# The low parts of the feed-forward down weights: a VectorE subtraction against a negated ScalarE copy and an adding DMA

## The chip, the cores and the metric

The kernel runs on one core of a Trainium2 chip. The metric is the device time of one execution in microseconds (us). In the names of the engines PE is TensorE (matmul), DVE is VectorE, ACT is ScalarE, POOL is GpSimd and SP is SyncE; "PEld" is the weight load of PE. DMAs are issued by SP, ACT or POOL, each with a queue of its own.

## What is computed

One inference step of a two-layer decoder trunk, for a prompt of 512 tokens and 8 sequences of 4 new tokens each, so 544 token columns in all. Layer 0 mixes tokens with a convolution module, layer 1 with stick-breaking attention. Each mixer is followed by the same gated feed-forward block, and that block is what the change touches:

```
def conv_ffn(h, past, w_gate, w_up, w_dw, b_dw, w_down):
    g = h @ w_gate
    ext = jnp.concatenate([past, g], axis=1)
    g_conv = causal_dwconv(ext, w_dw, b_dw)
    out = (jax.nn.silu(g_conv) * (h @ w_up)) @ w_down
    return out, ext[:, -(FFN_CONV_WIDTH - 1):]
```

The model width is 1024 (8 chunks of 128), the inner width D_FF is 2816 (22 chunks of 128). All data are float32.

## The kernel before

**Split products.** Each matrix product is made of two rounded parts per operand: `whi` is the weight rounded to the matmul format (a copy on ACT, line 369), `wlo` is the rest, weight minus `whi` (a subtraction on DVE, line 372). The activations have the same two parts (`XH`/`XL`, `TH`/`TL`, `HH`/`HL`). A product of one 128x128 block is then three matmuls: whi by high, whi by low, wlo by high. They stand on lines 459 to 461, 700 to 702, 1343 to 1345, 1543 to 1545 and 1970 to 1972.

**Weights.** A ring of two buffers `raw` holds 256 columns of a weight, loaded by a DMA from DRAM (line 332). From it `W.prep` makes one "slot" after another, a pair `whi`, `wlo` in a ring of five buffers. When a slot has been used, `W.free` drops it and prepares the slot five places on. When the last slot of a raw buffer has its `wlo`, the load of a new raw buffer is issued. In the program's listing below, slots carry their number: `whi74` and `wlo74` are slot 74.

**The feed-forward block.** `ffn(l, ...)` runs the 22 inner chunks in passes of 4, 6, 6 and 6 (`PASSES`). Within a pass the gates and ups of the next chunks alternate with the down products of the pass before. The gates and ups of the last three passes use four slots for two chunks ("a quad", kinds 0, 2, 3, 4 of the specs): a scheme with seven instead of eight block products, written in `products` (from line 1535 on):

```
mm(a, s1, 4, lambda: Tn(3), False, [("T", 1, 0), ("T", 1, 1)])
used(s1)
put("keep 22", a)
put("22", y)
mm(a, s2, 4, lambda: B(1, 1), False, bk(1, 1))
```

Each `mm` is 12 matmuls into one PSUM bank. The bank `a` goes on being added to, and its value is copied out in between: `put("keep 22", a)` is, for a gate, a copy of 240 columns and one of 32 columns (8x4) on ACT (lines 1579 and 1581), for an up one copy of 272 columns (line 1611). The next `mm` into `a` has to wait until that has been read. The down products use slots of kind 0 and 1 with 4 or 6 chunks (`nk`), and add to the residual on DVE (line 1634). Behind the block follows the last pass's down product: in layer 0 as `Wide.stream`, in layer 1 as `add_group`, both through `gemm` (lines 459 to 461).

**What sets the order.** Within the block the order is not the order of the code: each step is handed to `Plan.op` with an engine, a cost, and the names that it reads and writes. `Plan.run` then plays these costs through and emits the instructions in the order of that play, engine by engine. Each engine runs its own list strictly in that order. A matmul depends on `("slot", n)`, so the cost and place of the steps that write this name decide where the planner puts the matmuls. Waits for a DMA are told to the planner as steps on an engine of their own name, such as `raw{r}` with 5.0.

Of the kernel before, what the change touches and what calls it, by code (L numbers as in the profile page):

```python
# [13 lines left out]
AF = mybir.ActivationFunctionType  # L14
ALU = mybir.AluOpType
PSUM = bass.MemoryType.PSUM

P = 128
D = 1024
NC = D // P  # L20
# [18 lines left out]
SPLIT_BUFS = 5  # L39
# [185 lines left out]
def tile_trunk(  # L225
# [9 lines left out]
    dve, act, pool, pe = nc.vector, nc.scalar, nc.gpsimd, nc.tensor  # L235
# [20 lines left out]
    raws = []  # L256
# [59 lines left out]
    class Ring:  # L316
# [26 lines left out]
                nc.sync.dma_start(out=self.raw[self.nraw][:, k, cols], in_=src[:, k, cols])  # L343
            self.nraw += i

        def prep(self, later=None, halves=False):


            if self.nprep >= len(specs):
                return  # L350
            r, kind, last, nk = specs[self.nprep]
            more = self.more is not None
            home, bufs = (self.more, 1) if more else (ring, SPLIT_BUFS)
            i = self.nprep if more else ""
            hi = home.tile([P, NC, P], F32R, tag=f"whi{i}", name=f"whi{self.nprep}", bufs=bufs)
            lo = home.tile([P, NC, P], F32R, tag=f"wlo{i}", name=f"wlo{self.nprep}", bufs=bufs)
            self.w[self.nprep] = (hi, lo, nk)
            self.nprep += 1
            n = nk
            if kind < 2:  # L360
                src = self.raw[r][:, :nk, kind * P:(kind + 1) * P]
            elif kind == 4:
                n = nk // 2
                src = self.raw[r][:, n:, P:]
            else:
                src = self.sums[r].rearrange("p a k c -> p (a k) c") if kind == 2 else self.raw[r][:, :, 0:P]

            def high(k):
                act.copy(hi[:, k, :], src[:, k])  # L369

            def low(k=slice(0, n)):
                dve.tensor_tensor(lo[:, k, :], src[:, k], hi[:, k, :], op=ALU.subtract)  # L372
                if last:
                    del self.raw[r]
                    self.load()

            if halves:
                return [lambda f=f, k=k: f(k) for k in (slice(0, n // 2), slice(n // 2, n)) for f in (high, low)]
            high(slice(0, n))
            if later is None:  # L380
                low()
            else:
                later.insert(min(LATER, len(later)), low)
# [2 lines left out]
            del self.w[self.nfree]  # L386
            self.nfree += 1

        def free(self, later=None):
            self.drop()  # L390
            self.prep(later)

    W = Ring()

# [18 lines left out]
    def pcol(row, c):  # L413
        return prm[:, c, row:row + 1]
# [242 lines left out]
    for i in range(2):  # L657
        ch0 = (PE_CHUNKS[0] + i * len(PE_CHUNKS) // 2) * P
        for m in range(8):
            nj = min(4, CW - 4 * m)  # L660
            pool.dma_start(out=trow[i][m * n_g:(m + 1) * n_g, :nj * 32].rearrange("g (j h) -> g j h", j=nj),
                          in_=conv_w_dw[0, 4 * m:4 * m + nj, ch0:ch0 + n_g * 32].rearrange("j (g h) -> g j h", h=32))


    plan = Plan(E_CONV, 0.12)
# [382 lines left out]
    for c in range(0, NC, 2):  # L1048
# [9 lines left out]
        for cc in range(2):  # L1058
            plan.op("act", 0.33, lambda c=c, cc=cc, pt=pt: act.copy(
                ext_s[:, c + cc, :, 0:PAST], pt()[:, cc * 240:(cc + 1) * 240].rearrange("p (b t) -> p b t", b=NB)),  # L1060
                r=[pt, "junk"], w=[("past", c + cc)])
# [126 lines left out]
    for h, (c0, n) in enumerate(STREAMS):  # L1188
# [10 lines left out]
        if not h:  # L1199
# [6 lines left out]
    n = SA[1]  # L1206
    plan.op("pe", 0.53, lambda: pe.matmul(ms()[:, :n], mean_m, nrm.acc[0]()[:, :n], start=True, stop=True),
            r=[nrm.acc[0]], w=[ms])
    plan.op("act", 0.34, lambda: act.activation(rs()[:, :n], ms()[:, :n], AF.Sqrt, bias=eps_t[:, 0:1], scale=1.0),
            r=[ms, "table"], w=[rs])  # L1210
    plan.op("dve", 1.7, lambda: dve.reciprocal(rs()[:, :n], rs()[:, :n]), w=[rs])
    for c in range(NC):
# [3 lines left out]
                r=[rs, ("x", c, 0)], w=[u])  # L1216
        plan.op("act", 0.32, lambda c=c, u=u: act.activation(XH[:, c, 0:n], u()[:, :n], AF.Copy,
                                                             scale=pcol(R_FFN, c)), r=[u], w=[("XH", c, 0)])
        plan.op("dve", 0.37, lambda c=c, u=u: dve.scalar_tensor_tensor(
            XL[:, c, 0:n], u()[:, :n], pcol(R_FFN, c), XH[:, c, 0:n], op0=ALU.mult, op1=ALU.subtract),  # L1220
            r=[u, ("XH", c, 0)], w=[("XL", c, 0)], lift=NLIFT)
# [28 lines left out]
    def ffn(l, before, after):  # L1250
# [9 lines left out]
        plan = Plan(E_FFN)  # L1260
# [23 lines left out]
        def dcost(n):  # L1284
            return 0.06 + n * 1.06e-3

        def acost(n):
            return 0.04 + n * 0.885e-3


        def prepare(slot):

            r, kind, last, nk = specs[slot]
            src = [("raw", r)] if kind not in (2, 3) else [live[r]] if kind == 2 else [("S2", r)]
            low = []
            m = (nk * P) // (2 if kind == 4 else 1)
            plan.op("act", acost(m), lambda: W.free(low), r=src, w=[("slot", slot - SPLIT_BUFS), ("slot", slot), "prep"])
            plan.op("dve", dcost(m), lambda: low[0](), r=src, w=[("slot", slot), "low"])
            if last:
                plan.op(f"raw{r}", 5.0, lambda: None, w=[("raw", r + RAW_BUFS)], r=[("slot", slot), ("raw", r)])  # L1300

# [22 lines left out]
        def used(slot):  # L1324

            s = slot + SPLIT_BUFS
            if s >= len(specs):
                return
            r, kind, last, nk = specs[s]
            if kind == 0:  # L1330
                s_of[r] = s
            if kind == 2:
                live[r] = sums(r)
            prepare(s)
# [332 lines left out]
        for p0, pn in rest:  # L1667
# [9 lines left out]
            k0, nk = p0, pn  # L1677
# [7 lines left out]
        if l == 0:  # L1685
# [5 lines left out]
            last = Wide(HH, HL, evac, hold=HOLD)  # L1691
# [188 lines left out]
    def rows_q(j, bg):  # L1880
        rows = slice(j * HD, (j + 1) * HD)
        return rows, qT[rows, :, SEQ + 16 * bg:SEQ + 16 * bg + 16].rearrange("p c (b i) -> p c b i", b=4)
# [7 lines left out]
    for bg in range(2):  # L1890
        for j in range(2):
            rows, src = rows_q(j, bg)
# [28 lines left out]
    plan = Plan()  # L1921
# [40 lines left out]
    def weighted(pt, slot, h, q):  # L1962

        c0, n = (SA, SB)[h]

        def f():
            hi, lo, _ = W.w[slot]
            o = pt()[:, :n]
            for k in (2 * q, 2 * q + 1):
                pe.matmul(o, hi[:, k, :], XH[:, k, c0:c0 + n], start=(k == 0), stop=False)  # L1970
                pe.matmul(o, hi[:, k, :], XL[:, k, c0:c0 + n], start=False, stop=False)  # L1971
                pe.matmul(o, lo[:, k, :], XH[:, k, c0:c0 + n], start=False, stop=(k == NC - 1))  # L1972

        return f
# [353 lines left out]
    for i, tag in enumerate(("acc", "z", "z", "one")):  # L2328
        pt = psum(tag)
        begun.append(pt)  # L2330
        last = None
        for q in range(4):
            last = plan.op("pe", 6 * SA[1] * COL, weighted(pt, o0 + i, 0, q), w=[pt], follows=last,
                           r=[("slot", o0 + i)] + [("X", k) for k in (2 * q, 2 * q + 1)])
# [3 lines left out]
    for j in range(2):  # L2338
        rows = slice(j * HD, (j + 1) * HD)
        hi, lo = (X[rows, :, SEQ:T].rearrange("p c (b i) -> p c b i", b=NB) for X in (XH, XL))  # L2340
# [54 lines left out]
```

## Time and profile before

| | |
|---|---|
| median of 3 runs | 1292.23 us (1292.02 to 1292.42) |
| the profiled execution's own time | 1294.01 us |
| its span in the profile | 1292.0 us |
| PE busy | 1274.7 us (99%) |
| DVE busy | 981.1 us (76%) |
| ACT busy | 718.5 us (56%) |
| POOL busy | 158.5 us (12%) |
| read from HBM | 129.34 MB |

The profile is of one execution. Its span lies 2.0 us under that execution's own time, and that time 1.8 us over the median of the runs. Times in a timeline are microseconds from the span's start. Matmuls overlap, and their ends are modelled: a matmul's own duration is longer than the distance between the starts of two, so the distance is what counts for PE. The feed-forward block of layer 0 lies between about 225 and 558 us, that of layer 1 between about 905 and 1239 us.

### The profile page before, as it was taken

How to read it: one execution, taken by the hardware profiler on the slowest of the kernel's cores; microseconds unless marked ns; L12 is line 12 of the kernel's file. 1: busy time of each engine (PE TensorE's matmuls, PEld its weight loads, DVE VectorE, ACT ScalarE, POOL GpSimd, SP SyncE). 2: the span in 40 equal slices, each digit the busy share in tenths (PEclk: the TensorE clock that was granted, in tenths of full speed). 3: DMA queues.
4: the chain of work that ended last, by engine and by line, in shares of the span. 5: the costliest groups of instructions: out<-in, count | busy, mean ns of one | idle time of the engine just before them, and what ended most of it. 6: DMA issues, size and time to landing. Idle time of an engine off the chain costs nothing.

```text
span 1292.0 us, 26645 instructions
## 1 busy us (share of the span) xinstructions
PE 1274.7 (99%) x10908; PEld 1220.0 (94%) x10908; DVE 981.1 (76%) x1671; ACT 718.5 (56%) x1448; POOL 158.5 (12%) x301
## 2 busy tenths in 40 slices
PE   9999999999999999999999999999999999999997
PEld 8997789999999999999988988889999999999997
DVE  6899876988977887768356586756988987886864
ACT  6596574545654455445356587754645655455453
POOL 4000013111011010000142123100111011011000
PEclk9999999999999999999999999999999999999999
DMA  7464333123233233143544446333133233233221
GB/s 214 123 184 134 88 99 114 34 83 115 91 106 102 83 99 115 58 141 135 180 148 130 139 129 175 110 116 98 50 100 101 92 105 115 66 116 92 81 76 70
DMA packets 119308, 142.39 MB, mean 110 GB/s; under 512 B 5588, under 2 KB 110312, under 8 KB 118915
## 3 DMA queue, kind: packets, MB, share of 16 engines
q1 hardware_dynamic: 109871, 111.89, 28.0%
q0 software_dynamic: 9024, 28.78, 7.2%
q8 instruction: 86, 1.41, 0.5%
q14 instruction: 35, 0.29, 0.1%
q10 hardware_dynamic: 292, 0.02, 0.0%
HBM read 129.34 MB, written 12.18 MB: 110 GB/s over the span
## 4 chain that ended last, share of the span: by engine, by line
PE 92%; DVE 3%; issue 2%; ACT 1%; DMA 1%; DVEq 0%; POOL 0%; ACTq 0%; POOLq 0%; SPq 0%
PE acc L1545 5%; PE acc L1543 5%; PE acc L1544 5%; PE acc L700 4%; PE acc L701 4%; PE acc L702 4%; PE av L1343 3%; PE acc L460 3%; PE acc L459 3%; PE acc L461 3%; PE av L1344 3%; PE av L1345 3%; PE tr L1343 3%; PE tr L1344 3%; PE tr L1345 3%; PE tr L1545 3%
## 5 line engine op out<-in xcount | busy, mean ns | idle before, releaser
L372 DVE TENSOR_TENSOR wlo<-raw,whi 128x1024 fp32r<-128x1024 f32 (+2 forms) x245 | 257.4, 1052 | 45.0 <-ACT whi L369 43.2
L369 ACT CAST whi<-raw 128x1024 fp32r<-128x1024 f32 (+2 forms) x245 | 223.5, 914 | 115.3 <-PE tr L1344 21.7
L700 PE MATMUL acc<-XH,whi 128*128 128x288 f32 (+1 forms) x384 | 114.4, 298 | 0.0
L701 PE MATMUL acc<-XL,whi 128*128 128x288 f32 (+1 forms) x384 | 110.8, 288 | 0.0
L702 PE MATMUL acc<-XH,wlo 128*128 128x288 f32 (+1 forms) x384 | 110.3, 287 | 0.0
L1970 PE MATMUL acc<-XH,whi 128*128 128x256 f32 (+1 forms) x264 | 82.8, 314 | 0.6 <-ACT XH L2275 0.6
L1543 PE MATMUL acc<-TH,whi 128*128 128x272 f32 x288 | 82.9, 288 | 0.0
L1545 PE MATMUL acc<-TH,wlo 128*128 128x272 f32 x288 | 82.8, 288 | 0.0
L1544 PE MATMUL acc<-TL,whi 128*128 128x272 f32 x288 | 82.7, 287 | 0.0
L1579 ACT COPY G<-acc 128x272 f32<-128x272 f32 (+1 forms) x72 | 26.7, 371 | 95.2 <-PE acc L1545 95.2
L1971 PE MATMUL acc<-XL,whi 128*128 128x256 f32 (+1 forms) x264 | 76.2, 289 | 0.1
L1972 PE MATMUL acc<-XH,wlo 128*128 128x256 f32 (+1 forms) x264 | 75.9, 287 | 0.0
L700 PEld LDWEIGHTS acc<-XH,whi 128*128 128x128 f32 x384 | 72.3, 188 | 2.8 <-issue 1.6
L1343 PE MATMUL av<-HH,whi 128*128 128x288 f32 (+1 forms) x256 | 74.5, 291 | 0.0
L1344 PE MATMUL av<-HL,whi 128*128 128x288 f32 (+1 forms) x256 | 74.1, 290 | 0.0
L1345 PE MATMUL av<-HH,wlo 128*128 128x288 f32 (+1 forms) x256 | 73.9, 289 | 0.0
L1343 PE MATMUL tr<-HH,whi 128*128 128x256 f32 (+1 forms) x256 | 73.4, 287 | 0.0
L1344 PE MATMUL tr<-HL,whi 128*128 128x256 f32 (+1 forms) x256 | 73.3, 286 | 0.0
L1345 PE MATMUL tr<-HH,wlo 128*128 128x256 f32 (+1 forms) x256 | 72.9, 285 | 0.0
L701 PEld LDWEIGHTS acc<-XL,whi 128*128 128x128 f32 x384 | 72.3, 188 | 0.4
L702 PEld LDWEIGHTS acc<-XH,wlo 128*128 128x128 f32 x384 | 72.2, 188 | 0.0
L1484 DVE SCALAR_TENSOR_TENSOR cv<-G,fprm,cv 128x560 f32<-128x560 f32 x88 | 69.4, 796 | 0.5
(409 smaller groups left out, 4417.4 us busy)
## 6 DMA issues: line engine op xcount, KB each, us to landing
raw<-in_ffn_w_gate_dram SPq DMA_DIRECT2D x22, 1024.0 KB
raw<-in_ffn_w_up_dram SPq DMA_DIRECT2D x22, 1024.0 KB
raw<-in_ffn_w_down_dram SPq DMA_DIRECT2D x24, 768.0 KB
raw<-in_attn_w_qkv_dram SPq DMA_DIRECT2D x12, 1024.0 KB
raw<-in_conv_w_in_dram POOLq DMA_DIRECT2D x6, 1024.0 KB, 6.3
rep<-glu SPq DMA_DIRECT2D x36, 142.0 KB
raw<-in_conv_w_out_dram POOLq DMA_DIRECT2D x4, 1024.0 KB, 6.3
raw<-in_ffn_w_down_dram SPq DMA_DIRECT2D x8, 512.0 KB
```

Source lines behind the costliest of these rows:

```text
L369: act.copy(hi[:, k, :], src[:, k])
L372: dve.tensor_tensor(lo[:, k, :], src[:, k], hi[:, k, :], op=ALU.subtract)
L700: pe.matmul(o, hi[:, k, :], XH[:, k, c0:c0 + n], start=(k == 0), stop=False)
L701: pe.matmul(o, hi[:, k, :], XL[:, k, c0:c0 + n], start=False, stop=False)
L702: pe.matmul(o, lo[:, k, :], XH[:, k, c0:c0 + n], start=False, stop=(k == NC - 1))
L1343: pe.matmul(o, hi[:, j + k, :], xh, start=(start and k == 0), stop=False, **kw)
L1344: pe.matmul(o, hi[:, j + k, :], xl, start=False, stop=False, **kw)
L1345: pe.matmul(o, lo[:, j + k, :], xh, start=False, stop=(stop and k == len(xs) - 1), **kw)
L1543: pe.matmul(o, hi[:, j + k, :], xh, start=(start and k == 0), stop=False, **kw)
L1544: pe.matmul(o, hi[:, j + k, :], xl, start=False, stop=False, **kw)
L1545: pe.matmul(o, lo[:, j + k, :], xh, start=False, stop=(k == 3), **kw)
L1970: pe.matmul(o, hi[:, k, :], XH[:, k, c0:c0 + n], start=(k == 0), stop=False)
```

## The change

For the down slots (kind 0 or 1, fewer than 8 chunks) that are prepared within a feed-forward plan, `wlo` is no longer made on DVE. ACT writes the negated rounded weight into `wlo` (`minus`), and then a DMA on POOL's queue reads the weights from DRAM a second time and adds them to it (`rest`). There are 58 such slots, 29 in each layer: 8 of 512 columns (nk of 4) and 21 of 768 columns (nk of 6). The last three slots of each layer's last pass are prepared outside the plan and stay as they were. The raw buffer's next load is issued behind `minus` of its last slot. The planner is told of an ACT step at the cost of a copy, a POOL step of 1.2, and 5.0 on an engine of its own until the slot is there.

```diff
+            def minus():
+                act.activation(lo[:, :n, :], src, AF.Copy, scale=-1.0)
+                if last:
+                    del self.raw[r]
+                    self.load()
+
+            def rest():
+                pool.dma_start(out=lo[:, :n, :], in_=raws[r][0][:, :, kind * P:(kind + 1) * P], accum_op=ALU.add)
+
...
             high(slice(0, n))
+            if added:
+                later += [minus, rest]
+                return
...
-            plan.op("act", acost(m), lambda: W.free(low), r=src, w=[("slot", slot - SPLIT_BUFS), ("slot", slot), "prep"])
-            plan.op("dve", dcost(m), lambda: low[0](), r=src, w=[("slot", slot), "low"])
+            added = kind < 2 and nk < NC
+            plan.op("act", acost(m), lambda: W.free(low, added), r=src, w=[("slot", slot - SPLIT_BUFS), ("slot", slot), "prep"])
+            if added:
+                plan.op("act", acost(m), lambda: low[0](), r=src, w=[("slot", slot), "low"])
+                plan.op("pool", 1.2, lambda: low[1](), w=[("slot", slot)])
+                plan.op(f"low{slot}", 5.0, lambda: None, w=[("slot", slot)])
+            else:
+                plan.op("dve", dcost(m), lambda: low[0](), r=src, w=[("slot", slot), "low"])
```

Line numbers of the changed kernel are higher: by 18 in `ffn` (1543 is then 1561, 1343 is 1361, 1579 is 1597), by 12 between `Ring` and `ffn`, and `minus` and `rest` stand on lines 372 and 378.

The order moves with it on PE, ACT and POOL. First PE, in the gate quad of slots 70 to 73 (layer 0). Its bank `a` is `acc_310` before and `acc_313` after; `TH`, `TL` are the quad's combined inputs, `XH`, `XL` the block's inputs, `HH`, `HL` the inner activations of a down product. Before:

```order
L1543 MATMUL acc_310_4888<-TH0_3232,whi71_4854 128x272
L1544 MATMUL acc_310_4888<-TL0_3233,whi71_4854 128x272
L1545 MATMUL acc_310_4888<-TH0_3232,wlo71_4855 128x272
L1343 MATMUL tr_317_5026<-HH0_3038,whi74_4975 128x288
L1344 MATMUL tr_317_5026<-HL0_3039,whi74_4975 128x288
L1345 MATMUL tr_317_5026<-HH0_3038,wlo74_4976 128x288
...
L1543 MATMUL acc_310_4888<-XH_73,whi72_4876 128x272
L1544 MATMUL acc_310_4888<-XL_74,whi72_4876 128x272
L1545 MATMUL acc_310_4888<-XH_73,wlo72_4877 128x272
```

The same place now:

```order
L1561 MATMUL acc_313_4936<-TH0_3232,whi71_4841 128x272
L1562 MATMUL acc_313_4936<-TL0_3233,whi71_4841 128x272
L1563 MATMUL acc_313_4936<-TH0_3232,wlo71_4842 128x272
L1561 MATMUL acc_313_4936<-XH_73,whi72_4865 128x272
L1562 MATMUL acc_313_4936<-XL_74,whi72_4865 128x272
L1563 MATMUL acc_313_4936<-XH_73,wlo72_4866 128x272
...
L1561 MATMUL acc_316_5011<-TH0_3232,whi73_4910 128x272
L1562 MATMUL acc_316_5011<-TL0_3233,whi73_4910 128x272
L1563 MATMUL acc_316_5011<-TH0_3232,wlo73_4911 128x272
L1361 MATMUL tr_317_5079<-HH0_3038,whi74_4986 128x288
```

Between the group of slot 71 into the bank `a` and the group of slot 72 into the same bank stood the 18 matmuls of the down product of slot 74. They now come two groups of 12 later, and the two groups into `a` follow each other directly. The same holds in each layer for the second and third gate quad of the last two passes and the first two of the pass before them: six places in a layer. In the first gate quad of the last two passes a down product stood between them as well, and now six transposes of the state rows do. In the last up quad another group of 12, into the quad's third bank, stood there, and now four transposes and one matmul of slot 128 (272 in layer 1) do.

ACT, where slots 74 and 75 are prepared (`G_...<-acc` are the copies out of the bank `a`, 272 columns for "keep 21", 240 and 8x4 for "keep 22"). Before:

```order
L369 CAST whi74_4975<-raw29_4767 128x768
L1579 COPY G_314_4943<-acc_310_4888 128x272
L369 CAST whi75_5008<-raw29_4767 128x768
L1579 COPY G_314_4943<-acc_310_4888 128x240
L1581 COPY G_314_4943<-acc_310_4888 128x8x4
```

Now:

```order
L369 CAST whi74_4986<-raw29_4760 128x768
L372 ACTIVATE wlo74_4987<-raw29_4760 128x768
L369 CAST whi75_5003<-raw29_4760 128x768
L372 ACTIVATE wlo75_5004<-raw29_4760 128x768
L1597 COPY G_312_4924<-acc_313_4936 128x272
L1597 COPY G_312_4924<-acc_313_4936 128x240
L1599 COPY G_312_4924<-acc_313_4936 128x8x4
```

Each `whi` of these slots is followed at once by its negated copy, and the copies out of `a` come behind both pairs.

POOL, where the DMAs of slots 74 and 75 stand now (the copies `G<-fprm` fill in old gate rows, `SF<-G` save new ones):

```order
L1479 COPY G_311_4907<-fprm_76 128x8x2
L1479 COPY G_312_4924<-fprm_76 128x8x2
L378 DMA wlo74_4987<-in_ffn_w_down_dram 128x6x128
L378 DMA wlo75_5004<-in_ffn_w_down_dram 128x6x128
L1509 COPY SF0_3040<-G_311_4907 128x2
```

The two DMAs are new here, behind two copies that were there before and ahead of the saves.

More of the change, by code (lines that the diff above doesn't have):

```diff
@@ L344, in half, with prep @@
             self.nraw += i
-        def prep(self, later=None, halves=False):
+        def prep(self, later=None, halves=False, added=False):
             if self.nprep >= len(specs):
@@ L387, in drop, with free @@
             self.nfree += 1
-        def free(self, later=None):
+        def free(self, later=None, added=False):
             self.drop()
-            self.prep(later)
+            self.prep(later, added=added)
     W = Ring()
```

## The prediction

> **What bounds the kernel now.** I read the page first, for the shares of the engines.
>
> ```profile
> span 1292.0 us, 26645 instructions
> ...
> PE 1274.7 (99%) x10908; PEld 1220.0 (94%) x10908; DVE 981.1 (76%) x1671; ACT 718.5 (56%) x1448; POOL 158.5 (12%) x301
> ```
>
> PE leaves 17.3 us of the span. Nothing that is taken from DVE or given to ACT counts unless PE waits for it, so next come busy times by stretch: the two stretches of alternating products in the feed-forward blocks, and the 12 us behind the first.
>
> ```profile
> core 0: us, PE busy (x) PEld busy (x) DVE busy (x) ACT busy (x) POOL busy (x), PEclk, DMA share, GB/s
> 264.00:558.00 294.00, 294.00 (x2344) 293.66 (x2343) 238.72 (x381) 148.96 (x261) 22.13 (x64) 1.00 0.31 95
> 558.00:570.00 12.00, 11.03 (x91) 10.52 (x91) 8.63 (x15) 6.37 (x13) 2.04 (x4) 1.00 0.53 162
> ...
> 945.00:1239.00 294.00, 294.00 (x2344) 293.66 (x2343) 238.44 (x381) 148.92 (x261) 22.38 (x64) 1.00 0.30 95
> ```
>
> Where the change acts, PE is busy all 294 us: there is nothing to win there. Behind the block 1 us is open. The waits of PE say for what (what it waited for: us in total, times, longest):
>
> ```profile
> PE acc L460 <- DVE HL L1597: 1.4, 2, 0.7
> ...
> PE acc L459 <- DVE xT L1688: 1.1, 1, 1.1
> PE acc L461 <- DVE wlo L372: 0.7, 1, 0.7
> ...
> PE acc L459 <- ACT HH L1596: 0.5, 2, 0.3
> ```
>
> The first and last come once behind each block. All waits that this change could shorten are these 3.7 us. So the question is whether it opens new ones.
>
> **Work moved off and onto engines.** The groups with shapes kept apart:
>
> ```profile
> L372 DVE TENSOR_TENSOR wlo<-raw,whi 128x768 fp32r<-128x768 f32 x48 | 45.9, 956 | 9.3 <-ACT whi L369 9.0
> L372 DVE TENSOR_TENSOR wlo<-raw,whi 128x512 fp32r<-128x512 f32 x54 | 36.6, 684 | 4.7 <-ACT whi L369 4.1
> L369 ACT CAST whi<-raw 128x768 fp32r<-128x768 f32 x48 | 40.2, 837 | 33.9 <-PE acc L1544 17.5 <-PE av L1344 3.8 <-PE tr L1344 3.5
> L1481 ACT ACTIVATE cv<-G,fprm 128x560 f32<-128x560 f32 x44 | 37.6, 859 | 0.7
> ```
>
> DVE loses 42 x 0.956 + 16 x 0.684 = 51.1 us. ACT gains 58 negated copies. The trace has no such copy; the cast of the same size (0.84 us) bounds it below, the ACTIVATE of 560 columns scaled to 768 (1.18 us) above. I take 0.84, the same size. That is 42 x 0.84 and 16 of two thirds that, some 44 us more on ACT, which is 56% busy, and 58 issues on POOL, which is 12% busy. None of it is on the path by itself: PE's 294 us hide it, as long as each result comes before its matmul.
>
> **The order on PE: the main term.** In six places of each layer, the group into bank `a` whose value "keep 22" copies out, and the next group into `a`, now stand directly behind each other. A down product of 12 or 18 matmuls hid that copy before. How long a round trip over the same two copies is shows at the last group of a quad, where it is hidden. The timeline's rows (start, duration in us) of PE, then of ACT:
>
> ```profile
> 370.06 0.29 PE L1545 MATMUL acc<-XH,wlo 128*128 128x272 f32 x1
> 370.19 0.29 PE L1543 MATMUL acc<-TH,whi 128*128 128x272 f32 x1
> ...
> 371.69 0.28 PE L1343 MATMUL av<-HH,whi 128*128 128x256 f32 x1
> ```
>
> ```profile
> 370.39 0.36 ACT L1579 COPY G<-acc 128x240 f32<-128x240 f32 x1 [2.43 <-PE acc L1545]
> 370.64 0.19 ACT L1581 COPY G<-acc 128x32 f32<-128x32 f32 x1
> ```
>
> The last matmul into the bank starts at 370.06 and ends at 370.35. ACT starts 0.04 later and has read the bank at 370.83, that is 0.48 after PE's end. (12 matmuls take 371.69 - 370.19 = 1.50 us, 0.125 each.) How PE comes out of a wait is seen behind the block (PE, then DVE, then ACT):
>
> ```profile
> 558.19 0.60 PE L1645 MATMUL av<-ident,SF 128*18 128x128 f32 x4
> 558.63 0.38 PE L1645 MATMUL tr<-ident,SF 128*18 128x128 f32 x2
> 558.76 0.36 PE L459 MATMUL acc<-HH,whi 128*128 128x256 f32 x1
> ...
> 561.05 0.38 PE L459 MATMUL acc<-HH,whi 128*128 128x256 f32 x1 [0.27 <-ACT HH L1596]
> 562.14 0.39 PE L460 MATMUL acc<-HL,whi 128*128 128x256 f32 x1 [0.70 <-DVE HL L1597]
> 562.36 0.29 PE L461 MATMUL acc<-HH,wlo 128*128 128x256 f32 x1
> ```
>
> ```profile
> 559.04 0.44 DVE L1620 TENSOR_TENSOR h<-cv,h 128x272 f32<-128x272 f32 x1
> ...
> 560.49 0.96 DVE L372 TENSOR_TENSOR wlo<-raw,whi 128x768 fp32r<-128x768 f32 x1 [0.38 <-ACT whi L369]
> 561.36 0.72 DVE L1597 TENSOR_TENSOR HL<-h,HH 128x544 fp32r<-128x544 f32 x1
> ```
>
> ```profile
> 559.63 0.83 ACT L369 CAST whi<-raw 128x768 fp32r<-128x768 f32 x1
> 560.36 0.64 ACT L1596 CAST HH<-h 128x544 fp32r<-128x544 f32 x1
> ```
>
> `HL` ends at 562.08 and the matmul that waited starts at 562.14, 0.06 later; the one behind it follows after 0.22 instead of 0.12. So a bare bubble costs 0.29 (last matmul) + 0.48 + 0.06 - 0.125 (the usual distance) + 0.10 = 0.80 us. Twelve of them: **+9.6 us**. Nothing can hide them, since PE keeps its order.
>
> Four more places have six transposes in the gap. These take 558.76 - 558.19 = 0.57 us, which leaves 0.23 each: **+0.9 us**.
>
> Behind the block, the gap in the last up quad waits for one copy of 272 columns (0.39 us in the rows of that kind):
>
> ```profile
> L1611 ACT COPY h<-tr 128x272 f32<-128x272 f32 x30 | 11.6, 385 | 24.9 <-PE tr L1545 24.6
> ```
>
> It costs 0.29 + 0.04 + 0.39 + 0.06 - 0.125 + 0.10 = 0.75, of which four transposes (0.44) and a matmul (0.12) fill 0.56, work that then is missing later. On the other side `HH` no longer stands behind a `whi` cast on ACT (559.63, 0.83), and `HL` no longer behind a `wlo` on DVE (560.49, 0.96): `h` is ready at 559.48, ACT is free at about 559.7, so `HH` ends near 560.4 and `HL` near 561.1 instead of 562.08. The gain is 0.94 against a cost of 0.75: **-0.4 us** for both layers.
>
> **The landing of the new DMAs.** A wait is added on POOL (each DMA waits for its negated copy) with the copies and saves of gate rows and the state stores queued behind it; PE's transposes wait for the saves, but at the end of a pass only. What PE waits for is the landing. The nearest rows:
>
> ```profile
> raw<-in_conv_w_in_dram POOLq DMA_DIRECT2D x6, 1024.0 KB, 6.3
> out_dram<-h POOLq DMA_DIRECT2D x8, 32.0 KB, 1.8
> ```
>
> 384 KB lies at 1.8 + 4.5 x 352/992 = 3.4 us between them; if reading the destination as well doubles the part that grows with size, 5.0 us. No row shows an adding DMA, so the ends are 1.8 and twice the larger row, 12.6 us. I take 5.0. The time allowed comes from the order: the tightest slot (80, and 112, 224, 256) is freed five groups of 12, one bubble and two matmuls ahead of its first `wlo` matmul, 7.5 + 0.8 + 0.25 = 8.55 us. Cast and negated copy, one behind the other, and the handovers use 1.75, which leaves 6.8 us (6.5 if the copy takes 1.18). Slots 130 and 274 have about 7.2, slots like 68, 74 and 40 about 8.7 to 9.3, the rest more. At 5.0 the term is **0**; at 1.8 it is 0 too, since a landing that is early moves nothing on PE.
>
> The Trainium skill, "DMA: Bandwidth & Descriptors", section "Anatomy of one DMA", fits a DMA of this path with 2.0 us plus 1 us for every 436,000 bytes. By it 384 KB would land in 2.9 us and the sum stay the same; for 1024 KB it gives 4.4 where the row has 6.3, so the row decides.
>
> **The sum.** 9.6 + 0.9 - 0.4 + 0 = +10.1 us. The profiled execution took 1294.0 and would come to 1304.1; the median of the runs lies 1.8 below it, so the forecast is 1292.2 + 10.1 = **1302.3 us**. With a bubble of 0.65 to 1.0 us (ACT between the two copies, or ACT not idle when PE ends) the twelve give 7.8 to 12, so its own range is 1299 to 1306. What a measurement can tell from no change is 0.2%, 2.6 us.
>
> **Rivals.** *The DMAs land late.* They read DRAM in 512-byte rows beside raw loads released by the same negated copy. At 9.0 us slots 80 and 112 come 2.2 late each, 130 by 1.8, four others by 0.1 to 0.3: about 7 per layer, +14, so 1316. It decides from 6.8 us. At 12.6 some ten slots of a layer are late by 1.5 to 5.8, the sum is near +84, 1376. Against it: 6.3 us for a transfer 2.7 times as large. Chance 0.20, of which two thirds within 1318.
>
> *The bubbles let the clock fall.* If the group of 12 (1.50 us) behind each bubble ran at half speed, that is 12 x 1.5 = 18 us on top: 1320. The stretch 558 to 570 has two such waits at a clock of 1.00, which speaks against it. The Trainium skill, "TensorE: Matmul & The Clock Gate", section "A second HAM failure mode: psum-queue depth-cycling", tells of a kernel where short idle times between groups had this effect. Chance 0.03.
>
> *DVE's relief is what counts.* It ends faster: with the subtractions gone, DVE's and ACT's waits above go (3.7 us, and 0.1 for each of six restarts), 4.3 in all, 1288. That needs bubbles under 0.1 us each, that is, a copy that ends while the matmul before it still runs; the rows put ACT's start behind PE's end. Chance 0.05. With bubbles between 0.1 and about 0.3 us gains and losses cancel within 2.6 us: 1292, chance 0.06.
>
> **How the numbers follow.** The forecast keeps 0.66. Faster 0.05, same 0.06, slower 0.66 + 0.20 + 0.03 = 0.89. The range goes from 1297 (bubbles of 0.5) to 1318, which holds late landings up to about 9 us; left out are faster and same (0.11), later landings (0.07) and the clock.
>
> **What would show it.** Right: PE gets waits on lines 1561 to 1563 for the copy on line 1599, twelve of about 0.5 us each as the profile counts idle time (from PE's modelled end), and PE's idle time grows by about 7 us, since the waits' other parts are hidden in overlapping durations; the stretches of 294 us get about 5 us longer each; no wait for `wlo` on line 378; `HL`'s wait of 0.7 behind each block goes. Wrong: those stretches keep 294 us, or PE waits for DMAs into `wlo`, or the clock drops under 1.00 in the blocks.

## The result and the profile after

The changed kernel takes 1328.1 us (median of 4 runs, 1325.5 to 1332.6) against 1292.3 (1292.0 to 1293.3): slower by 35.8 us, ratio 1.0276 [1.0254, 1.0299]. The forecast was +10.1 us with a range up to 1318. The direction was right, the size was not. Two of the four runs took 1325.5 and 1325.6 us, the other two 1330.6 and 1332.6 at a lower mean granted clock (0.990 against 0.995 and 0.993). The profiled execution is the one of 1325.6 us. Its page:

```profile
span 1323.7 us, 26816 instructions
...
PE 1285.9 (97%) x10908; PEld 1225.0 (93%) x10908; DVE 935.1 (71%) x1613; ACT 759.6 (57%) x1506; POOL 254.0 (19%) x359
```

The span grew by 31.7 us. PE's idle time grew from 17.3 to 37.8 us, and PE's busy time by 11.2 us with the same 10908 matmuls. So there are two things to look for: waits, and matmuls that became slower. DVE lost 46.0 us (51.1 was worked out), which gained nothing for the kernel. The two stretches of alternating products, in which PE never idled before:

```profile
264.00:558.00 294.00, 285.53 (x2245) 282.81 (x2244) 209.82 (x341) 157.43 (x270) 57.50 (x85) 0.99 0.52 117
945.00:1240.00 295.00, 287.25 (x2256) 284.64 (x2255) 212.43 (x347) 160.80 (x284) 64.39 (x94) 0.99 0.54 121
```

PE idles 8.5 and 7.8 us in them, the granted clock is 0.99 instead of 1.00, and the DMA engines are busy 0.52 and 0.54 of the time instead of some 0.30. The waits of PE (in total, times, longest):

```profile
PE acc L1561 <- ACT G L1599: 6.4, 12, 0.5
PE tr L1363 <- DMA wlo<-in_ffn_w_down_dram: 6.0, 3, 2.7
PE acc L473 <- DMA wlo<-in_ffn_w_down_dram: 5.6, 4, 3.1
...
PE av L1363 <- DMA wlo<-in_ffn_w_down_dram: 3.7, 2, 2.8
...
PE acc L472 <- DVE HL L1615: 0.4, 2, 0.2
```

The first row is the twelve bubbles as forecast. The next three were forecast not to be there: nine waits for an adding DMA, 15.3 us. The last row is the relief of `HL` (1.4 before). How long an adding DMA takes from issue to landing (median, last column), and what a negated copy and an issue take:

```profile
wlo<-in_ffn_w_down_dram POOLq DMA_DIRECT2D x42, 384.0 KB, 9.3
...
wlo<-in_ffn_w_down_dram POOLq DMA_DIRECT2D x16, 256.0 KB, 6.1
```

```profile
L378 POOL DMA_DIRECT2D wlo<-in_ffn_w_down_dram x58 | 83.7, 1462 | 295.1 <-ACT wlo L372 264.4 <-ACT whi L369 9.3 <-ACT G L1522 6.8
L372 ACT ACTIVATE wlo<-raw 128x768 fp32r<-128x768 f32 x42 | 35.4, 842 | 0.0
```

The copy is 0.842 us, as taken (0.84). The landing is 9.3 us where 5.0 was taken. And the matmuls that became slower stand behind the long waits (stretches of the same view as above; the last three columns are granted clock, DMA share, GB/s):

```profile
510.00:516.00 6.00, 3.23 (x24) 2.80 (x23) 0.51 (x2) 4.40 (x9) 2.20 (x3) 1.00 1.16 233
516.00:520.00 4.00, 3.50 (x18) 3.50 (x19) 0.06 (x1) 0.29 (x1) 1.31 (x5) 0.62 1.39 203
...
582.00:590.00 8.00, 6.67 (x37) 6.38 (x36) 2.47 (x5) 2.51 (x5) 0.00 (x0) 0.58 0.70 210
```

A bubble and most of a wait of 2.7 us for slot 112 lie in 510 to 516, at full clock. In the next 4 us the clock is 0.62 on average. From 582 to 590, behind the wait for slot 131 (3.1 us) and around that for slot 132 (1.3 us), it is 0.58. Counted by the starts of the matmuls, 15 of them behind slot 112's wait stand 0.21 to 0.23 us apart instead of 0.12 to 0.125, 15 behind that of slot 224 and 22 around those of slots 131 and 132: 1.4, 1.5 and 2.0 us more, 4.9 us together.

The theory from here on: the order costs the bubbles, some 10 us. The other 25 us are late landings and the clock behind them. Landings are late because two adding DMAs are in flight at once, beside the raw load that the second slot's negated copy releases. The rivals: that the order itself costs more, that adding is slow by itself, that the delay is in the issue, or that the planner was told a wrong number.

### The profile page after: what moved, and what is told of

It reads as the page before. It is cut to its first block, busy times and chain, and to the rows that moved or that the text cites. A ratio compares the mean times of both kernels' runs of the same rounds, so it can differ in the third digit from the quotient of the medians.

```text
span 1323.7 us, 26816 instructions
## 1 busy us (share of the span) xinstructions
PE 1285.9 (97%) x10908; PEld 1225.0 (93%) x10908; DVE 935.1 (71%) x1613; ACT 759.6 (57%) x1506; POOL 254.0 (19%) x359
## 4 chain that ended last, share of the span: by engine, by line
PE 85%; DMA 5%; DVE 5%; issue 2%; ACT 2%; POOL 0%; DVEq 0%; ACTq 0%; POOLq 0%
DMA wlo<-in_ffn_w_down_dram 5%; PE acc L1561 4%; PE acc L1563 4%; PE acc L1562 4%; PE acc L712 4%; PE acc L713 3%; PE acc L714 3%; PE av L1363 3%; PE av L1361 3%; PE tr L1363 3%; PE av L1362 3%; PE tr L1361 3%; PE tr L1362 3%; PE acc L473 3%; PE acc L471 3%; PE acc L472 3%
## 5 line engine op out<-in xcount | busy, mean ns | idle before, releaser
L381 DVE TENSOR_TENSOR wlo<-raw,whi 128x1024 fp32r<-128x1024 f32 (+2 forms) x187 | 206.7, 1106 | 41.1 <-ACT whi L369 39.5
L378 POOL DMA_DIRECT2D wlo<-in_ffn_w_down_dram x58 | 83.7, 1462 | 295.1 <-ACT wlo L372 264.4
```

Of the source, the lines that this page charges most:

```text
L378: pool.dma_start(out=lo[:, :n, :], in_=raws[r][0][:, :, kind * P:(kind + 1) * P], accum_op=ALU.add)
```

## The experiments

Each ratio is against the kernel before on the same chip.

**1. The order alone.** The subtraction stands in the place of the DMA; PE's order is that of the changed kernel.

```diff
-                later += [minus, rest]
+                later += [lambda: None, low]
```

> The changed kernel's order on PE, unchanged in every instruction, but the low parts come from the VectorE subtraction again, issued at the place of the DMA. Theory (the order costs the twelve bubbles, the rest of the loss is the late landing of the adding DMAs): 1302 us, 1300 to 1305, twelve waits of 0.5 us for the copies out of the bank, no wait for wlo, granted clock 1.00. Rival (the order itself costs nearly all of it, by what the bubbles do to the clock and to the engines behind them): 1320 to 1328 us.

Measured: 1313.3 us, ratio 1.0161 [1.0146, 1.0177]: neither. The waits of PE:

```profile
PE acc L1561 <- ACT G L1599: 6.4, 12, 0.5
PE av L1361 <- ACT h L1670: 3.9, 2, 1.9
...
PE acc L472 <- DVE HL L1615: 1.8, 2, 0.9
```

The bubbles are there. The second row is new in this run alone: at 271 and 962 us PE waits 1.9 us for a copy of state rows. That copy stands on ACT behind a cast of `HH`, which waits for `h` from DVE (2.4 us of ACT idle before that cast at 272 us, by the timeline; in the changed kernel, where DVE has fewer subtractions, 0.3). Behind these two waits 15 and 13 matmuls are 0.20 to 0.24 us apart, 3.1 us more together. These waits, the slower matmuls and the longer wait for `HL` make up most of what lies over 1303. So this run shows the bubbles, but it doesn't isolate them. The second run of experiment 8 comes closer.

**2. A plain copy of the same bytes.**

```diff
-                pool.dma_start(out=lo[:, :n, :], in_=raws[r][0][:, :, kind * P:(kind + 1) * P], accum_op=ALU.add)
+                pool.dma_start(out=lo[:, :n, :], in_=raws[r][0][:, :, kind * P:(kind + 1) * P])
```

> The changed kernel with a DMA that overwrites instead of adding: same bytes, same pieces, same order on every engine, the low part is then the whole weight. Theory A (adding doubles a 512-byte piece from some 33 to 65 ns on its DMA engine, and this makes two transfers in flight land after 9 us instead of some 6): pieces near 33 ns, landing of 384 KB near 6 us, one or two waits for wlo of under 1 us, 1303 to 1307 us. Theory B (512-byte rows fetched a second time beside the raw loads are that slow whether added or not): pieces near 65 ns, landing 9.3 us, 1325 to 1330 us.

Measured: 1304.7 us, ratio 1.0086 [1.0070, 1.0101]. Landing, and the row of software queue 0 (packets, MB, share of 16 engines), then the wait that is left:

```profile
q0 software_dynamic: 50400, 49.49, 16.7%
...
wlo<-in_ffn_w_down_dram POOLq DMA_DIRECT2D x42, 384.0 KB, 6.0
```

```profile
PE acc L473 <- DMA wlo<-in_ffn_w_down_dram: 1.4, 2, 1.0
```

Theory A holds in its result: with 6.0 us of landing all but two short waits go, and the kernel stands 11.6 us over the one before. Its price of a piece was off. The queue's row in the other two kernels, before and then after:

```profile
q0 software_dynamic: 9024, 28.78, 7.2%
```

```profile
q0 software_dynamic: 50400, 49.49, 19.7%
```

The 41376 new pieces (packets of 512 bytes) took (0.197 x 1323.7 - 0.072 x 1292.0) x 16 / 41376 = 65 ns each on their DMA engine when added, and (0.167 x 1303.3 - 0.072 x 1292.0) x 16 / 41376 = 48 ns when copied. Adding costs a third more per piece, not twice, and its issue on POOL takes 1.46 us against 0.81 for the copy. With both, the first transfer of a pair lands after 7.7 to 9.3 us in the changed kernel and after 3.9 to 4.2 here (slots 74, 80, 106, 112 and 224 in both). The packets around slot 74 show why. The copy has moved 606 of its 768 pieces when the raw load starts. The added transfer has moved 148 by then and shares the engines with it from there on: 152 pieces per microsecond while the raw load moves 150 of its own, against 360 alone.

**3. Half the bytes added.**

```diff
-                pool.dma_start(out=lo[:, :n, :], in_=raws[r][0][:, :, kind * P:(kind + 1) * P], accum_op=ALU.add)
+                pool.dma_start(out=lo[:, :n // 2, :], in_=raws[r][0][:, :n // 2, kind * P:(kind + 1) * P], accum_op=ALU.add)
```

> The changed kernel with a DMA that adds only the first half of the chunks of each slot (192 KB or 128 KB), so that half of each low part stays the negated high part. Theory (landing = about 2.2 us until the first piece + 65 ns for each of the pieces queued on an engine, own and partner's, + the raw load's share): 2.2 + 1.6 + 1.6 + up to 2 = 5.5 to 7 us, nearly no wait for wlo, 1303 to 1306 us. Rival (the delay is fixed: waiting for ScalarE's copy, the issue on GpSimd, the time to start): landing stays above 8 us, 1318 us or more.

Measured: 1303.2 us, ratio 1.0077 [1.0062, 1.0093], landing:

```profile
wlo<-in_ffn_w_down_dram POOLq DMA_DIRECT2D x42, 192.0 KB, 5.4
```

It is still an adding DMA with an issue of 1.29 us, and the waits for it come to 1.2 us. So there is no fixed delay of an adding DMA or of its issue that makes it late; the time grows with the bytes that are added.

**4. The order of before, with one DMA of each pair.** The planner is told of the subtraction, as before; what is emitted in its place is the negated copy and the DMA.

```diff
-            added = kind < 2 and nk < NC
+            added = kind == 1 and nk < NC
...
-            if added:
-                plan.op("act", acost(m), lambda: low[0](), r=src, w=[("slot", slot), "low"])
-                plan.op("pool", 1.2, lambda: low[1](), w=[("slot", slot)])
-                plan.op(f"low{slot}", 5.0, lambda: None, w=[("slot", slot)])
-            else:
-                plan.op("dve", dcost(m), lambda: low[0](), r=src, w=[("slot", slot), "low"])
+            plan.op("dve", dcost(m), lambda: [f() for f in low], r=src, w=[("slot", slot), "low"])
```

> The order of the kernel before on PE, unchanged; only the second slot of each pair (28 of 58) gets its low part from the negated copy and the DMA. These slots have 10.8 to 20 us from their release to their first wlo matmul, except 129, 131, 273, 275 with 9.2. Theory (a single 384 KB transfer lands in 5.3 us alone, 6 to 8 us beside a raw load; with cast, copy and handovers 2.3 us more): no wait except up to 1 us at those four; no bubbles; 1291 to 1295 us. Rival (the adding DMAs cost through something else than their time of landing, such as the clock or contention with the raw loads): 1300 us or more.

Measured: 1292.8 us, ratio 1.0000 [0.9991, 1.0009] (11 runs). No wait for a DMA is left among PE's waits, and the landing of a lone 384 KB is

```profile
wlo<-in_ffn_w_down_dram POOLq DMA_DIRECT2D x20, 384.0 KB, 7.2
```

Two things follow. One adding DMA of a pair, with 9 us or more from the slot's release to its first `wlo` matmul, costs nothing beside the raw loads. And taking 28 subtractions from DVE (its busy time falls by 23 us) gains nothing either: the rival of DVE's relief is out.

**5. The order of before, all 58 slots by DMA.** As experiment 4, with `added` for both slots of a pair, as in the change.

> The order of the kernel before on PE, unchanged, but all 58 slots get their low part from the negated copy and the adding DMA. No bubbles, but six slots of a layer have only 6 to 8 us, and one 3, from their release to their first wlo matmul. Theory (2.3 us for cast, copy and handovers, then 6 to 8 us of landing): seven to ten waits for wlo in a layer of 1.5 to 4 us, each of 1.9 us or more followed by some 1.4 us of a lowered clock, 1330 to 1360 us. Rival (landing is near the 5.0 us that the planner is told, and what cost time in the changed kernel was its order): 1300 to 1312 us.

Measured: 1354.7 us, ratio 1.0479 [1.0463, 1.0495].

```profile
PE av L1358 <- DMA wlo<-in_ffn_w_down_dram: 20.1, 10, 3.8
PE tr L1358 <- DMA wlo<-in_ffn_w_down_dram: 14.2, 6, 5.1
PE acc L473 <- DMA wlo<-in_ffn_w_down_dram: 4.8, 5, 2.0
```

This lies in the expected range: 21 waits, 39 us, no bubbles. So the moved order, with all its bubbles, saves time for this DMA: without it the change would have cost 62 us.

**6. The planner is told 9.0.**

```diff
-                plan.op(f"low{slot}", 5.0, lambda: None, w=[("slot", slot)])
+                plan.op(f"low{slot}", 9.0, lambda: None, w=[("slot", slot)])
```

> The changed kernel, with the planner told 9.0 instead of 5.0 for the landing of an adding DMA; it moves the products on PE. Most down slots then have 12 us or more from release to first wlo matmul, but slots 80, 112, 224 and 256 fall to 6.2, the slots behind the block stay at 8.4 to 11.4, and there are 18 bare bubbles instead of 12. Theory: bubbles 18 x 0.83 = 15 us, four waits of some 4 us with the clock lowered behind each (22 us), the waits behind the blocks as in the changed kernel (10 us): 1330 to 1345 us. Rival (the number told was the fault, and the true one mends it): 1300 to 1312 us.

Measured: 1315.5 us, ratio 1.0170 [1.0154, 1.0186]: between the two ranges, in neither.

```profile
PE acc L473 <- DMA wlo<-in_ffn_w_down_dram: 5.3, 3, 2.8
PE acc L1561 <- ACT G L1597: 3.3, 6, 0.6
```

The 18 bubbles came (12 and these 6). The four waits of 4 us at slots 80, 112, 224 and 256 did not, only one of 0.3. Two bubbles now lie in the time that slots 80 and 224 have (at 407 and 410 us, and at 1103 and 1106), which I had left out, and the transfers of 224 and 256 land after 6.2 and 6.1 us, before the raw load. The number told was a fault worth some 13 us, but the true one doesn't mend the bubbles or the end of the block.

**7. The raw load behind the adding DMAs.** Only the queue and place of the raw loads that these slots release are changed.

```diff
-        def load(self):
+        def load(self, queue=None):
...
-            (pool if self.nraw < CONV_RAWS else nc.sync).dma_start(out=t[:, :nk, :], in_=src)
+            (queue or (pool if self.nraw < CONV_RAWS else nc.sync)).dma_start(out=t[:, :nk, :], in_=src)
...
             def minus():
                 act.activation(lo[:, :n, :], src, AF.Copy, scale=-1.0)
                 if last:
                     del self.raw[r]
-                    self.load()
 
             def rest():
                 pool.dma_start(out=lo[:, :n, :], in_=raws[r][0][:, :, kind * P:(kind + 1) * P], accum_op=ALU.add)
+                if last:
+                    self.load(pool)
```

> The changed kernel, same order on PE, ScalarE and VectorE; the only edit is that the raw load which the second slot of a pair releases is no longer issued on SyncE's queue at once but on GpSimd's queue, behind the adding DMA of that slot. Theory (a transfer lands late because a raw load that is released in the same microsecond takes every other turn of the 16 DMA engines, and the pair's second transfer stands behind the first): with the raw load behind both, the first of a pair lands 4.5 to 5 us and the second 6 to 7 us after its issue, nearly no wait for wlo, granted clock back near 1.00, 1303 to 1307 us. Rival (adding is slow by itself, 65 ns a piece and 1.4 us of issue, and sharing has little part): waits for wlo stay, 1318 us or more.

Measured: 1311.3 us, ratio 1.0141 [1.0125, 1.0156], over the expected range.

```profile
wlo<-in_ffn_w_down_dram POOLq DMA_DIRECT2D x42, 384.0 KB, 6.4
```

```profile
PE acc L474 <- DMA wlo<-in_ffn_w_down_dram: 4.1, 1, 4.1
...
PE yt L1760 <- ACT xg L1745: 1.4, 1, 1.4
```

In the pairs of 384 KB inside the blocks the first transfer now lands after 5.5 to 5.8 us and the second after 6.1 to 7.7; where a pair follows close behind another (slots 82, 114, 226 and 258) it is 7.2 to 7.5 and 7.6 to 8.9. Inside the blocks no wait for `wlo` is left: without the sharing with the raw load these transfers are in time. The surplus over 1303 is in waits that the edit itself made or lengthened. Slot 132's DMA now stands on POOL's queue behind the raw load of slot 131, and PE waits 4.1 us for it, with 26 matmuls 0.21 us apart behind. And at the end of layer 1's block a raw load lands 8.3 us after its issue on that queue, where it took 4.4 on SP's in the changed kernel; ACT waits 1.1 us for it with a cast, and `xg`, for which PE waits in the second row, stands behind that cast.

**8. The end of the block apart.** In the first run the ten slots 128 to 132 and 272 to 276 are subtracted, at the DMA's place. The second run has experiment 7's edit on top.

```diff
-                later += [minus, rest]
+                tail = self.nprep - 1 in (*range(128, 133), *range(272, 277))
+                later += [lambda: None, low] if tail else [minus, rest]
```

> The changed kernel, same order on PE, but the ten slots that are used at and behind the end of a block (128 to 132, 272 to 276) get their low parts from the subtraction again, issued at the DMA's place; the other 48 keep the adding DMA, and the raw loads stay on SyncE's queue. Theory (late landing inside the blocks: the five waits of the changed kernel at slots 68, 80, 112, 224, 256, 9.8 us, and some 3 to 4 us of lowered clock behind those of 112 and 224, on top of the bubbles' 10): 1313 to 1319 us. Rival (what is lost beyond the bubbles lies behind the blocks alone): 1302 to 1305 us.

> The same as the run before, and the raw loads that the slots with an adding DMA release are issued behind that DMA on GpSimd's queue. Theory (with the raw loads out of the way no DMA is late inside the blocks, and behind them there is none): only the twelve bubbles and the waits of the kernel before are left, granted clock 1.00 in the blocks, 1301 to 1304 us, which is what the first forecast gave for the whole change. Rival (adding itself or a load on GpSimd's queue costs something more): 1307 us or more.

Measured: 1318.5 us, ratio 1.0192 [1.0175, 1.0209], and 1305.7 us, ratio 1.0096 [1.0079, 1.0113]. The second stands 1.7 us over its expected range and under the rival's. The waits of the first, then of the second:

```profile
PE acc L1562 <- ACT G L1600: 6.4, 12, 0.5
PE tr L1364 <- DMA wlo<-in_ffn_w_down_dram: 6.1, 3, 2.9
PE av L1364 <- DMA wlo<-in_ffn_w_down_dram: 3.8, 2, 2.8
```

```profile
PE acc L1563 <- ACT G L1601: 6.4, 12, 0.5
...
PE acc L474 <- DVE HL L1617: 1.8, 2, 0.9
...
PE tr L1365 <- DMA wlo<-in_ffn_w_down_dram: 0.5, 1, 0.5
```

These two runs split the 35.8 us by their ratios: 12.4 us for the order with its bubbles (1.0096, with a longer wait for `HL` in it, 1.8 against 0.4 us), 12.4 us for late landings inside the blocks with their clock (1.0192 against 1.0096), and 10.9 us for late landings behind the blocks (1.0276 against 1.0192). Each part has an uncertainty of some 2 to 4 us, from the intervals.

**9. A version that is a little faster than both.** The kernel before, with the subtraction of slots 132 and 276 put behind the last `HH` and `HL`; nothing of the change is in it.

```diff
-            plan.op("dve", dcost(m), lambda: low[0](), r=src, w=[("slot", slot), "low"])
+            plan.op("dve", dcost(m), lambda: low[0](), r=src, w=[("slot", slot), "low"], lift=-2.0 if slot in (132, 276) else 0.0)
```

> The kernel before with one edit that has nothing of the change: in slots 132 and 276 the low part's subtraction, and with it the cast, are put behind the last HH and HL steps of the block on ScalarE and VectorE. In the kernel before HL waits behind that cast and that subtraction, and PE waits for it 0.3 and 0.7 us at the end of each block. PE's order is unchanged. Theory: these waits go but for some 0.2 us, 0.7 to 1.2 us per block less: 1290 to 1291.5 us. Rival (the time is lost again at the next wait behind the block): 1292 to 1293 us.

Measured: 1291.4 us, ratio 0.9985 [0.9976, 0.9994] (11 runs).

```profile
PE acc L460 <- DVE HL L1597: 0.4, 2, 0.2
```

The wait for `HL` goes from 1.4 to 0.4 us and that for `HH` is no longer in the list. The gain is 0.15%, and its interval leaves out 1. The relief of `HL` and `HH` that the change brought is had by moving one subtraction of each layer, and with it one cast.

## Why the prediction was wrong

**The bubbles: right.** Twelve waits on lines 1561 to 1563, 0.54 us each in the profile. One of them, PE and then ACT:

```profile
387.39 0.29 PE L1563 MATMUL acc<-TH,wlo 128*128 128x272 f32 x1
388.21 0.39 PE L1561 MATMUL acc<-XH,whi 128*128 128x272 f32 x1 [0.54 <-ACT G L1599]
388.44 0.29 PE L1562 MATMUL acc<-XL,whi 128*128 128x272 f32 x1
```

```profile
387.71 0.36 ACT L1597 COPY G<-acc 128x240 f32<-128x240 f32 x1 [2.54 <-PE acc L1563]
387.97 0.19 ACT L1599 COPY G<-acc 128x32 f32<-128x32 f32 x1
```

From start to start 0.82 us instead of 0.125, and 0.23 instead of 0.125 behind it: 0.80, which is the price that was worked out. Four gaps with transposes were to cost 0.9 us; there is no such wait. `HL`'s relief came, and the kernel with fast landings (experiment 2) stands 11.6 us over the one before, where +10.1 was forecast for landings in time.

**The landing: the step that failed.** It is the term "taken 5.0, 0 us", worth 23 us by the split of experiment 8. An adding transfer that hardly meets another does land near it: slot 272 after 6.0 us, slot 224 in experiment 6 after 6.2. But the step priced one transfer by rows of other transfers and put nothing beside it. Here two are issued 1.5 us apart, and the second slot's negated copy releases a raw load of 0.75 or 1 MB in between. With these the median is 9.3 us, and slots 80, 112, 224 and 256, which had 6.8, landed after 7.7, 9.3, 9.3 and 8.4. The Trainium skill, "DMA: Bandwidth & Descriptors", section "Anatomy of one DMA", failed in the same way by its 2.9 us: a fit for one transfer doesn't hold beside others.

**The rival "the DMAs land late": the right mechanism, mis-sized.** It named the raw loads that the same copy releases, took 9.0 us and came to 14 us of waits, 1316. The waits were 15.3 us, at slots 68, 80, 112, 131 and 132 of layer 0 and 224, 256, 274 and 275 of layer 1. That the sum is so close is luck in part: slot 80 was late by 0.9 us and not 2.2, slot 130 not at all where 1.8 was given, and slots 131 and 132, late by 3.1 and 1.3, were not among those named. By landing less wait, slot 68 had 7.7 us where 8.7 to 9.3 was worked out, and slot 131 had 7.2 where it was counted among those with more. What the rival lacked is the price behind a wait.

**The clock: the wrong place.** The rival let it fall behind the bubbles. It does not: behind 0.54 us of idle time the clock stays at 1.00 (510 to 516 above), and twelve bubbles alone leave the mean clock at 0.999 in the second run of experiment 8. It falls behind the long waits for DMAs, which had been priced at their length alone; the 4.9 us of slower matmuls counted above are that price in the profiled execution.

## What to carry to other kernels

A transfer's time to land is priced with what the same step releases beside it: the partner of the pair and the load that the freed buffer sets off. A long wait on PE can cost more than its length: here the matmuls behind most waits of 1.9 us or more ran at half clock for a while, and the twelve short waits, far apart, cost their length and restart alone. Moving work off an engine that PE hardly waits for gained nothing here. What then decides is whether the order leaves enough time for the new latency, and the planner has to be told the latency beside the other transfers (9.0 instead of 5.0 was worth some 13 us).

## What was not expected of the hardware

**Where the clock falls.** After the first 10 us of the kernel, no wait of PE from 1.0 to 1.73 us that stood by itself was followed by more than 3 slow matmuls, in all the runs here (over twenty such waits). Of the 17 waits from 1.92 to 5.1 us, 15 were followed by 8 to 26 matmuls at 0.20 to 0.24 us. Short waits close together can do it too: in experiment 5 three of 0.69, 0.61 and 0.14 us between 890.9 and 894.0 us were followed by 15 slow matmuls, and in no other run were they. It is not a fixed rule: in the first run of experiment 8 two waits of 2.8 and 2.9 us, at 1105 and 515 us, ended differently.

```profile
1108.00:1112.00 4.00, 3.65 (x29) 3.65 (x30) 1.14 (x2) 0.10 (x1) 1.11 (x5) 1.00 1.38 203
517.00:521.00 4.00, 3.33 (x15) 3.33 (x16) 0.00 (x0) 0.32 (x1) 1.34 (x5) 0.50 1.39 202
```

Full clock behind the one, half behind the other. In the traces' own record the granted clock is 1.0 or 0.5 and nothing between, and each time it falls, but for the last at the end of a kernel, it is 0.5 for 3.41 us or for twice that. In the changed kernel these stretches are the following (slots 112, 131 with 132, and 224):

```profile
517.00:520.40 3.40, 3.40 (x19) 3.40 (x18) 0.46 (x2) 0.00 (x0) 0.31 (x3) 0.50 1.35 212
581.85:588.65 6.80, 5.47 (x26) 5.17 (x25) 1.72 (x3) 2.40 (x4) 0.00 (x0) 0.50 0.85 253
1114.35:1117.70 3.35, 3.35 (x17) 3.35 (x17) 1.13 (x2) 0.00 (x0) 0.00 (x0) 0.50 1.31 229
```

The Trainium skill, "TensorE: Matmul & The Clock Gate", section "Part 1: The HAM clock gate (the "warmup" mystery)", tells of exactly two rates, half and full, and of a free-running activity window of about 3.4 us, with half rate after an idle one. The two rates and the length agree with the traces. A window that runs on its own could explain why equal waits differ; no run here tests that. A wait of 1.92 us is shorter than the idle window that the page names, and the half clock behind it is measured. No run here separated the clock's price from that of the waits; 1.4 to 2.4 us per period is counted from the starts of matmuls.

**An adding DMA** took 65 ns for a 512-byte piece on average where a plain copy of the same piece took 48, and 1.46 us to issue on POOL where the copy took 0.81.
